# Six up-projection steps of each feed-forward layer, done as seven products of quarters

## The chip, the cores and the metric

The kernel runs on one core of one Trainium2 chip. The metric is the device time of one execution in microseconds (us), as a median over runs; a profiled execution gives the trace, in which every instruction of the five engines has its start and its duration. PE is TensorE (matrix products), DVE is VectorE, ACT is ScalarE, POOL is GpSimd, and SP is SyncE, which here issues most DMA transfers.

## The reference

One inference step of a two-layer decoder trunk for 512 prompt tokens, 16 learned tokens in front of them, and 8 x 4 tokens of a sample group. Each layer is a mixer (linear attention with RWKV-7 in layer 0, gated DeltaNet in layer 1) and a feed-forward block, each followed by a layer norm. The change touches the feed-forward block alone:

```
x <- LN(alpha*x + ConvFFN(x))
ConvFFN: W_down( silu(causal_dwconv3(x W_gate)) * (x W_up) )
D_MODEL = 1024    D_FF = 2816    FFN_CONV = 3
```

## The kernel before

The block of a layer is written by `ffn`. Features lie on the 128 partitions and tokens along the free axis: 560 columns in layer 0, 548 in layer 1. D_FF is worked through in 22 steps f of 128 features, and these in three parts (`PARTS`): f = 0 to 7, 8 to 15, 16 to 21. A step computes `pg` (the gate) and `pu` (the up projection) of x. Matrix products are made in three terms, since each operand is held as a high and a low half: `xh`, `xl` for x, `wh`, `wl` for a weight (`split`: the high half by a cast on ACT, the low half by a subtraction, as a rule on DVE). A projection is thus 8 tiles along the 1024 inputs x 3 terms x 2 halves of the columns = 48 matmuls. Its weights come by one DMA of 512 KB into a `wraw` tile; `fetch` has three of these slots, and SP's next fetch waits for the slot of the third one back to be read.

After the products of a step, ACT copies `pg` from PSUM to `gp`; three DVE instructions make the convolution (`ac`), ACT the tanh (`th`), DVE the rest of silu and the product with `pu` (`h`), and ACT and DVE split it into `hh` and `hl`. POOL copies the carried rows in and out (`cn`, `gp`). After each part the down projection adds up over the part's features: 8 output tiles `pd` of 48 matmuls each, which DVE adds into the residual `r`. After part 0, POOL sums the tiles of `r`, and in step f = 12 a mean is taken off them (8 POOL subtractions). Up to four PSUM tiles of two banks each are in use. The first two steps' products are made inside the layer norm before (`lead`; their weights are `vh`, `vl`), so that pg and pu of f = 2 are the first ones that `ffn` issues itself.

Order on each engine is set by a scheduler that goes by priority, in the order of the code; `later` and the new `sooner` shift that priority.

Of the kernel before, what the change touches and what calls it, by code (L numbers as in the profile page):

```python
# [12 lines left out]
F32 = mybir.dt.float32  # L13
# [8 lines left out]
KT = 8  # L22
# [26 lines left out]
class K:  # L49
    def __init__(self, ctx, tc, a, o):  # L50
        self.ctx, self.tc, self.nc, self.a, self.o = ctx, tc, tc.nc, a, o
        self.cp = ctx.enter_context(tc.tile_pool(name="const", bufs=1))
        self.table = False
        self.rp = ctx.enter_context(tc.tile_pool(name="rp", bufs=1))
        self.wp = ctx.enter_context(tc.tile_pool(name="wp", bufs=2))
        self.nw, self.every = 0, 1
        self.cut = KT
        self.side, self.rate, self.credit, self.pre, self.raw, self.lo = None, 0, 0, [], [], None

    def consts(self):  # L60
# [66 lines left out]
    def weights(self, src, k):  # L127
        return self.pre.pop(0) if self.pre else self.prepared(src, k)
# [218 lines left out]
def h2(ap, n=280):  # L347
    return ap.rearrange("p (h c) -> p h c", c=n)
# [14 lines left out]
LAST = Span(12)  # L363


def ffn(k, l, sn, xh, xl, r, pp, lead, nxt):
    nc, tc = k.nc, k.tc
    P, N, C, G = sn.pr, sn.nt, sn.c, sn.pr + 2
    E = G + 46
    with ExitStack() as es:  # L370
        sp = es.enter_context(tc.tile_pool(name=f"ffn{l}", bufs=2))
        hp = es.enter_context(tc.tile_pool(name=f"ffnh{l}", bufs=1))
        cs = hp.tile([128, NFF, 8, 2], F32, name="cs")
        nc.scalar.dma_start(cs, k.a["s_ffn"][l])
        cn = hp.tile([128, NFF, 9, 2], F32, name="cn")
        hh = hp.tile([128, KT, N], F32R, name="hh")
        hl = hp.tile([128, KT, N], F32R, name="hl")
        ln = LN(k, es, f"f{l}", sp, pp, r, sn)
        for f0, nf in PARTS:
            for j in range(nf):  # L380
                f = f0 + j
                if f == PARTS[1][0] + 4:
                    pc = pp.tile([128, 2, 512], F32, tag="pj", name="pc")
                    for i, (c, m) in enumerate(sn.halves):
                        nc.tensor.matmul(pc[:, i, 0:m], k.o1024, total[:, c : c + m], start=True, stop=True)
                    nc.scalar.copy(h2(total, sn.w), pc[:, :, 0 : sn.w])
                    for m in range(KT):
                        nc.gpsimd.tensor_sub(r[:, m, 0:N], r[:, m, 0:N], total)
                if lead:
# [15 lines left out]
                nc.vector.tensor_scalar(ac[:, 0:E], gp[:, 0:E], w(0), k.v(f"fb{l}", f), op0=ALU.mult, op1=ALU.add)  # L405
# [8 lines left out]
                nc.vector.scalar_tensor_tensor(  # L414
                    h2(h[:, 0:P], C), h2(th[:, 0:P], C), 0.5, pu[:, :, 0:C], op0=ALU.mult, op1=ALU.mult
                )
                nc.vector.scalar_tensor_tensor(
                    h[:, P:N].rearrange("p (b c) -> p b c", c=4),
                    th[:, G : G + 48].rearrange("p (b c) -> p b c", c=6)[:, :, 0:4], 0.5,
                    pu[:, 1, C : C + NS].rearrange("p (b c) -> p b c", c=4), op0=ALU.mult, op1=ALU.mult,  # L420
                )
                k.split(h, hh[:, j], hl[:, j])
            src = lambda m: k.a["w_down"][l, m][:, f0 : f0 + nf]
            if f0 + nf < NFF:
                for m in range(KT):
# [36 lines left out]
class LN:  # L462
# [58 lines left out]
    def add(self, h, s, p, ps):  # L521
        k, nc, r, w = self.k, self.k.nc, self.r, self.sn.w
        x = r[:, 2 * p : 2 * p + 2, s]
        nc.vector.scalar_tensor_tensor(x, x, self.alpha, ps[:, :, 0:w], op0=ALU.mult, op1=ALU.add)
        if p == 1:
            nc.gpsimd.tensor_add(self.sum, r[:, 0:2, s], x)
            (q0, _), (q1, _) = self.square(s, 0), self.square(s, 1)
            nc.vector.tensor_add(self.sq[h], q0, q1)
        elif p == 2:
            nc.gpsimd.tensor_add(self.sum, self.sum, x)  # L530
            nc.vector.tensor_add(self.sq[h], self.sq[h], self.square(s, p)[0])
            nc.gpsimd.tensor_add(self.sum[:, 0], self.sum[:, 0], self.sum[:, 1])
            nc.vector.tensor_add(self.sq[h][:, 0], self.sq[h][:, 0], self.sq[h][:, 1])
# [1427 lines left out]
```

## Time and profile before

| | |
|---|---|
| median of 3 runs | 1909.08 us (1909.01 to 1911.29) |
| profiled execution, its own time | 1901.78 us |
| its span in the trace | 1900.0 us |
| PE busy | 1794.4 us, 94% |
| DVE, ACT, POOL busy | 62%, 40%, 25% |

The span runs from the first to the last instruction of the trace; the 1.8 us beside it lie around the program. The profiled execution is 7.3 us shorter than the median of the other runs, so sums are made as differences and then put on the median. The steps that `ffn` issues itself and the down projections of parts 0 and 1 lie at 567 to 916 us of the span in layer 0 and at 1502 to 1847 us in layer 1.

### The profile page before, as it was taken

Reading aid. Unit: us, or ns where it says so; the run is one execution under the profiler, and the core shown is the slowest. Engines: PE = TensorE matmul, PEld = TensorE weight load, DVE = VectorE, ACT = ScalarE, POOL = GpSimd, SP = SyncE. Lnnn points to the kernel's source line nnn. Section 1 sums busy time; section 2 is a strip of 40 time slices with the busy share of each in tenths; the row PEclk is TensorE's granted clock in tenths of the full one; section 3 lists DMA queues with packets and bytes.
Section 4 is the critical chain, followed back from the end, with each engine's and each line's share of the span. In section 5 each row is a group of like instructions: output and inputs, shape, how many; then the busy total and the mean of one; then the engine's idle time right before and its main releaser. Section 6 shows DMA issues by size and latency. Waiting matters only on the chain.

```text
span 1900.0 us, 34370 instructions
## 1 busy us (share of the span) xinstructions
PE 1794.4 (94%) x13901; PEld 1679.7 (88%) x13901; DVE 1184.1 (62%) x2047; ACT 754.7 (40%) x1393; POOL 482.4 (25%) x750
## 2 busy tenths in 40 slices
PE   8999999798899999999988999899978999999997
PEld 7887888676899999999987997898768999999996
DVE  5757444546785556535766887688578654564466
ACT  6453423435353223223446454444344432232233
POOL 1333343313430113000131433333143201130002
PEclk9999999889899999999998999899898999999998
DMA  6110222301412222323321112421333122222231
GB/s 208 45 45 25 59 84 65 118 23 40 163 52 78 79 89 78 90 89 92 116 72 54 65 40 73 138 64 47 103 122 100 49 80 88 89 82 86 90 105 48
DMA packets 67358, 153.64 MB, mean 81 GB/s; under 512 B 15656, under 2 KB 26728, under 8 KB 67200
## 3 DMA queue, kind: packets, MB, share of 16 engines
q1 hardware_dynamic: 62784, 142.68, 24.3%
q10 hardware_dynamic: 3104, 4.15, 0.7%
q0 software_dynamic: 1312, 4.63, 0.6%
q8 instruction: 109, 1.79, 0.4%
q14 instruction: 49, 0.40, 0.1%
HBM read 136.72 MB, written 14.70 MB: 80 GB/s over the span
## 4 chain that ended last, share of the span: by engine, by line
PE 79%; DVE 9%; issue 4%; ACT 4%; DMA 2%; POOL 2%; SPq 0%; POOLq 0%; DVEq 0%; ACTq 0%
PE pd L162 17%; PE pu L162 13%; PE pg L162 13%; PE ph L162 12%; PE lead L162 3%; PE p L786 2%; PE pm L952 2%; PE px L740 1%; PE pw L756 1%; PE psr L286 1%; PE pt L750 1%; DVE ac L1534 1%; DVE r L566 1%; DVE r L1909 1%; PE psm L259 1%
## 5 line engine op out<-in xcount | busy, mean ns | idle before, releaser
L109 ACT CAST wh<-wraw 128x1024 fp32r<-128x1024 f32 x177 | 185.0, 1045 | 442.4 <-issue 156.2
L110 DVE TENSOR_TENSOR wl<-wraw,wh 128x1024 fp32r<-128x1024 f32 x156 | 210.0, 1346 | 177.6 <-ACT wh L109 177.1
L162 PE MATMUL ph<-xh,wh 128*128 128x280 f32 (+3 forms) x864 | 266.8, 309 | 9.4 <-ACT wh L109 6.1
L162 PE MATMUL ph<-xh,wl 128*128 128x280 f32 (+3 forms) x864 | 264.1, 306 | 0.4 <-DVE wl L110 0.4
L162 PE MATMUL ph<-xl,wh 128*128 128x280 f32 (+3 forms) x864 | 263.8, 306 | 0.0
L162 PE MATMUL pg<-xh,wh 128*128 128x264 f32 (+3 forms) x640 | 186.6, 292 | 0.0
L162 PE MATMUL pu<-xh,wl 128*128 128x264 f32 (+3 forms) x640 | 186.4, 291 | 0.0
L162 PE MATMUL pg<-xh,wl 128*128 128x264 f32 (+3 forms) x640 | 186.4, 291 | 0.0
L162 PE MATMUL pu<-xh,wh 128*128 128x264 f32 (+3 forms) x640 | 186.2, 291 | 0.0
L162 PE MATMUL pu<-xl,wh 128*128 128x264 f32 (+3 forms) x640 | 186.0, 291 | 0.0
L162 PE MATMUL pg<-xl,wh 128*128 128x264 f32 (+3 forms) x640 | 186.0, 291 | 0.0
L162 PEld LDWEIGHTS ph<-xh,wh 128*128 128x128 f32 x864 | 166.8, 193 | 16.9 <-ACT wh L109 7.2
L162 PEld LDWEIGHTS ph<-xl,wh 128*128 128x128 f32 x864 | 166.7, 193 | 5.6 <-issue 3.6
L162 PEld LDWEIGHTS ph<-xh,wl 128*128 128x128 f32 x864 | 166.4, 193 | 5.0 <-issue 3.6
L162 PE MATMUL pd<-hl,wh 128*128 128x280 f32 (+1 forms) x512 | 148.8, 291 | 0.1
L162 PE MATMUL pd<-hh,wl 128*128 128x280 f32 (+1 forms) x512 | 148.7, 291 | 0.0
L162 PE MATMUL pd<-hh,wh 128*128 128x280 f32 (+1 forms) x512 | 147.9, 290 | 0.0
L401 POOL COPY cn<-gp 128x2 f32<-128x2 f32 x44 | 31.1, 707 | 437.4 <-ACT gp L399 437.4
L162 PEld LDWEIGHTS pg<-xl,wh 128*128 128x128 f32 x640 | 121.0, 189 | 0.1
L162 PEld LDWEIGHTS pu<-xl,wh 128*128 128x128 f32 x640 | 121.0, 189 | 0.0
L162 PEld LDWEIGHTS pg<-xh,wh 128*128 128x128 f32 x640 | 120.9, 189 | 0.1
L162 PEld LDWEIGHTS pu<-xh,wh 128*128 128x128 f32 x640 | 120.9, 189 | 0.0
(566 smaller groups left out, 4751.0 us busy)
## 6 DMA issues: line engine op xcount, KB each, us to landing
wraw<-in_w_up SPq DMA_DIRECT2D x88, 512.0 KB, 3.5
wraw<-in_w_down SPq DMA_DIRECT2D x32, 512.0 KB, 3.5
wraw<-in_w_c SPq DMA_DIRECT2D x32, 512.0 KB, 3.6
wraw<-in_w_ab SPq DMA_DIRECT2D x26, 512.0 KB, 3.7
wraw<-in_w_down SPq DMA_DIRECT2D x16, 384.0 KB, 3.3
wraw<-in_w_oab SPq DMA_DIRECT2D x8, 512.0 KB, 4.0
sb<-in_s_gdn SPq DMA_DIRECT2D x16, 256.0 KB, 2.7
so<-in_s_gdn SPq DMA_DIRECT2D x16, 256.0 KB, 3.0
```

What stands on the lines that cost most here:

```text
L109: self.nc.scalar.copy(hi, src)
L110: (eng or self.nc.vector).tensor_sub(lo, src, hi.bitcast(F32))
L162: self.nc.tensor.matmul(ps[:, :m], a[:, i, :], x[:, i, c : c + m], start=(i == 0 and n == 0), stop=(i == k - 1 and n == 2))
L259: last = self.nc.tensor.matmul(ps[:, :m], lhsT, rhs[:, c : c + m], start=True, stop=True)
L286: k.nc.tensor.matmul(ps, z[:, 64 * b : 64 * b + 64], s[:, b % 4], start=(b == 0), stop=(b == 7))
L401: nc.gpsimd.tensor_copy(cn[:, f, 0, :], gp[:, P:G])
L566: st(t, t, k.v(g, m), rs, op0=ALU.mult, op1=ALU.mult)
L740: nc.tensor.matmul(px[:L, i, :L], a16[:L, i, :L], T[:L, i, :L], start=True, stop=True)
L750: nc.tensor.matmul(pt[:L, i, :L], W[:L, i, :L], X[:L, i, :L], start=not ta, stop=True)
L756: nc.tensor.matmul(pw[:L, i, :L], X[:L, i, :L], W[:L, i, :L], start=not wa, stop=True)
L786: nc.tensor.matmul(t[:L, i:e], a(h0 + i), y, start=(j == 0), stop=(j == len(terms) - 1))
L952: mm(pms[h][:L, n, :, :L], x[hs, tl], d["ra"][hs, :, tl], start=True, stop=True)
```

## The change

From f = 5 on, every other step of parts 0 and 1 (f = 5, 7, 9, 11, 13, 15, in each layer) no longer calls `proj` for `pg` and `pu`. The weights of gate and up projection form a 2 x 2 matrix of blocks (two outputs by two halves of the 1024 inputs), and x one of 2 x 2 blocks (two halves of the inputs by two halves of the columns). Strassen's scheme in Winograd's form makes the product of the two with seven block products in place of eight. A block product is 4 tiles x 3 terms = 12 matmuls of 280 columns (274 in layer 1), in a PSUM tile `pv` of its own. What the scheme needs beside them:

- once a layer (`sums`, emitted behind step f = 2): four differences of quarters of x, in two pieces each: 8 POOL instructions of 128x560, 8 ACT casts, and 8 low halves, 4 each on DVE and POOL;
- for each such step (`weights`): four sums or differences of half weights on POOL (128x512), 7 high halves on ACT, 6 low halves on DVE and one on POOL;
- for each such step (`products`): the seven tiles are emptied by 2 ACT copies and 6 DVE additions (the one behind the sixth product in two pieces), with 2 more additions on POOL, all at a priority 400 earlier (`sooner`).

The first tap of the convolution goes from DVE to ACT in these steps. The sums over `r` are now made after part 1 in place of part 0, in a tile `k.mid`, and the mean is taken off in step f = 18 in place of f = 12; the layer norm's pools are opened after part 1.

```diff
+    @contextmanager
+    def sooner(self):
+
+        tc = self.tc
+        p = tc.cur_priority
+        tc.cur_priority = p - 400
+        yield
+        tc.cur_priority = p
...
+    def sums(self):
...
+        ts = [tuple(self.xp.tile([128, 4, w], F32R, name=f"x{n}{i}") for n in "hl") for i in range(4)]
+        for j in (0, 2):
+            y = lambda a, b: x(a, b)[:, j : j + 2]
+
+            def diff(i, eng, p, q):
+                t = self.sp.tile([128, 2, 280], F32, tag="sum", name="xt")[:, :, 0:w]
+                eng.tensor_sub(t, p, q)
+                k.split(t, *(p[:, j : j + 2] for p in ts[i]), nc.gpsimd if i % 2 else None)
+                return t
+
+            t1 = diff(0, nc.gpsimd, y(0, 1), y(0, 0))
+            t2 = diff(1, nc.gpsimd, y(1, 1), t1)
+            diff(2, nc.gpsimd, y(1, 1), y(0, 1))
+            diff(3, nc.gpsimd, y(1, 0), t2)
...
+        s1 = both(True, h(u, 0), h(u, 1))
+        a11, c2 = room()
+        k.split(h(g, 0), *a11)
+        s2 = both(False, s1, h(g, 0))
+        k.split(s2, *c2)
+        a12, c1 = room()
+        k.split(h(g, 1), *a12, gp)
+        k.split(s1, *c1)
+        s4 = both(False, h(g, 1), s2)
+        s3 = both(False, h(g, 0), h(u, 0))
+        c3, c4 = room()
+        k.split(s3, *c3)
+        k.split(s4, *c4)
+        a22, = room(1)
+        k.split(h(u, 1), *a22)
...
+        def product(wt, xt):
+            ps = pp.tile([128, 2, 512], F32, tag="pj", name="pv")[:, 0, 0:w]
+            terms = [(wt[a][:, i], xt[b][:, i]) for i in range(4) for a, b in ((0, 0), (0, 1), (1, 0))]
+            for n, (p, q) in enumerate(terms):
+                nc.tensor.matmul(ps, p, q, start=n == 0, stop=n == 11)
+            return ps
...
+        ps = product(a11, self.b11)
+        with k.sooner():
+            nc.scalar.copy(c11, ps)
+        ps = product(s2, t2)
+        with k.sooner():
+            add(u2, ps, c11)
...
+        ps = product(a22, t4)
+        with k.sooner():
+            add(u3, ps, u3)
...
-                if f == PARTS[1][0] + 4:
+                if f == PARTS[2][0] + 2:
...
+                seven = SV <= f < PARTS[2][0] and f % 2
...
+                if f == 2:
+                    sv.sums()
```

ACT's order where `ffn` of layer 0 begins, before the change. `gp<-lead`, `th` and `hh` belong to f = 0 and 1; the `wh` in the last row but two is the high half for pg of f = 3.

```order
L246 ACTIVATE th<-ac 128x576
L399 COPY gp<-lead 128x528
L400 COPY gp<-lead 128x8x4
L109 CAST hh<-h 128x560
L246 ACTIVATE th<-ac 128x576
L109 CAST hh<-h 128x560
L109 CAST wh<-wraw 128x1024
L399 COPY gp<-pg 128x528
L400 COPY gp<-pg 128x8x4
```

The same place with the change; `xt` are the differences of x that POOL makes, `xh_65..` their high halves.

```order
L119 CAST hh<-h 128x560
L119 CAST xh_6513<-xt 128x560
L256 ACTIVATE th<-ac 128x576
L119 CAST xh_6515<-xt 128x560
L119 CAST xh_6517<-xt 128x560
L119 CAST xh_6519<-xt 128x560
L119 CAST hh<-h 128x560
L119 CAST xh_6513<-xt 128x560
L119 CAST xh_6515<-xt 128x560
L119 CAST xh_6517<-xt 128x560
L119 CAST wh<-wraw 128x1024
L531 COPY gp<-pg 128x528
```

Seven casts of differences now stand ahead of the weights' cast for pg of f = 3, one of them ahead of the tanh of f = 1 and six behind it. On POOL, the differences and low halves stand at that place in this order (nothing like them stood there before, only the four small rows of copies per step):

```order
L401 TENSOR_TENSOR xt<-r,xt 128x560
L401 TENSOR_TENSOR xt<-r 128x560
L528 MEMSET gp 128x2
L529 COPY gp<-cs 128x8x2
L401 TENSOR_TENSOR xt<-r,xt 128x560
L120 TENSOR_TENSOR xl_6516<-xt,xh_6515 128x560
L401 TENSOR_TENSOR xt<-r 128x560
L120 TENSOR_TENSOR xl_6520<-xt,xh_6519 128x560
L401 TENSOR_TENSOR xt<-r,xt 128x560
L401 TENSOR_TENSOR xt<-r 128x560
L120 TENSOR_TENSOR xl_6516<-xt,xh_6515 128x560
L401 TENSOR_TENSOR xt<-r,xt 128x560
```

One more difference, the first, stands ahead of these rows; the last row but two is the ninth of the large ones, counted with it, and its cast is the last that ACT makes ahead of the weights of f = 3.

DVE's order in part 1 of layer 0, before the change: one normal step, from the low half of the weights to that of h.

```order
L110 TENSOR_TENSOR wl<-wraw,wh 128x1024
L405 TENSOR_SCALAR ac<-gp,vec 128x576
L407 SCALAR_TENSOR_TENSOR ac<-gp,vec,ac 128x576 x2
L412 SCALAR_TENSOR_TENSOR th<-th,ac 128x576
L414 SCALAR_TENSOR_TENSOR h<-th,pu 128x528
L417 SCALAR_TENSOR_TENSOR h<-th,pu 128x32
L110 TENSOR_TENSOR wl<-wraw,wh 128x1024
L110 TENSOR_TENSOR hl<-h,hh 128x560
```

The same stretch with the change, from the end of a normal step (f = 12) into the following step of seven (f = 13). The rows with 128x512 are low halves for the seven products, those with `pv` empty their tiles.

```order
L120 TENSOR_TENSOR wl<-ws,wh 128x512 x2
L120 TENSOR_TENSOR hl<-h,hh 128x560
L464 TENSOR_TENSOR u_8434<-pv,gp 128x280
L120 TENSOR_TENSOR wl<-wraw,wh 128x1024
L467 TENSOR_TENSOR gp<-pv,gp 128x280
L473 TENSOR_TENSOR u_8436<-pv,u_8434 128x280
L478 TENSOR_TENSOR gp<-pv,u_8434 128x248
L478 TENSOR_TENSOR gp<-pv,u_8434 128x8x4
L120 TENSOR_TENSOR wl<-ws,wh 128x512
L120 TENSOR_TENSOR wl<-wraw,wh 128x1024
L482 TENSOR_TENSOR u_8436<-pv,u_8436 128x280
L542 SCALAR_TENSOR_TENSOR ac<-gp,vec,ac 128x576
```

A pair of steps thus keeps its two long `wl` rows and gets six short ones and six additions from PSUM for the two long rows and the tensor-scalar row that the step of seven drops; the `wl` of the next pg (fourth row) now stands behind the first addition, and so behind the second product.

## Rows read from the trace of the kernel before

**Rows 1.** The page: span, busy time by engine.

```profile
span 1900.0 us, 34370 instructions
PE 1794.4 (94%) x13901; PEld 1679.7 (88%) x13901; DVE 1184.1 (62%) x2047; ACT 754.7 (40%) x1393; POOL 482.4 (25%) x750
```

**Rows 2.** Stretches of both blocks: PE, PEld, DVE, ACT, POOL busy, PEclk, DMA.

```profile
567.00:916.00 349.00, 348.97 (x2699) 348.34 (x2698) 185.59 (x221) 101.10 (x144) 44.60 (x93) 1.00 0.29 89
1502.00:1847.00 345.00, 344.96 (x2701) 344.35 (x2700) 183.96 (x219) 99.64 (x144) 44.30 (x93) 1.00 0.29 88
```

**Rows 3.** The chain that ended last: start, duration, piece.

```profile
567.16 6.21 PE pg L162 x48
...
579.58 6.21 PE pg L162 x48
...
641.64 2.94 PE pd L162 x23
...
644.60 46.63 PE pd L162 x361
...
1578.94 46.28 PE pd L162 x361
...
1643.56 6.12 PE pu L162 x48
```

**Rows 4.** Timeline of ACT and DVE where the block of layer 0 begins.

```profile
573.31 1.05 ACT L109 CAST wh<-wraw 128x1024 fp32r<-128x1024 f32 x1 [2.28 <-PE pg L162]
574.39 1.23 DVE L110 TENSOR_TENSOR wl<-wraw,wh 128x1024 fp32r<-128x1024 f32 x1 [2.58 <-ACT wh L109]
576.15 1.67 DVE L407 SCALAR_TENSOR_TENSOR ac<-gp,vec,ac 128x576 f32<-128x576 f32 x2
578.57 0.76 DVE L412 SCALAR_TENSOR_TENSOR th<-th,ac 128x576 f32<-128x576 f32 x1 [0.75 <-ACT th L246]
```

**Rows 5.** Timeline of POOL and DVE around step f = 12 and in part 0's end.

```profile
692.14 1.39 POOL L434 TENSOR_TENSOR lnsum<-lnsum,r 128x560 f32<-128x560 f32 x1 [4.78 <-DVE r L429]
692.22 2.40 DVE L110 TENSOR_TENSOR wl<-wraw,wh 128x1024 fp32r<-128x1024 f32 x1 [0.22 <-ACT wh L109]
...
743.03 13.16 POOL L388 TENSOR_TENSOR r<-r,lnsum 128x560 f32<-128x560 f32 x8 [3.55 <-ACT lnsum L386]
...
749.05 2.46 DVE L110 TENSOR_TENSOR wl<-wraw,wh 128x1024 fp32r<-128x1024 f32 x1 [5.28 <-ACT wh L109]
751.43 1.64 DVE L405 TENSOR_SCALAR ac<-gp,vec 128x576 f32<-128x576 f32 x1
753.11 3.70 DVE L407 SCALAR_TENSOR_TENSOR ac<-gp,vec,ac 128x576 f32<-128x576 f32 x2
```

**Rows 6.** Groups by shape: busy us, mean ns of one; and DMA issues of the page.

```profile
L109 ACT CAST hh<-h 128x560 fp32r<-128x560 f32 x20 | 13.1, 655 | 3.3 <-DVE h L417 3.3
L1742 POOL TENSOR_TENSOR so<-so,egs 128x512 f32<-128x512 f32 x16 | 17.8, 1127 | 26.8 <-DMA so<-in_s_gdn 12.2 <-DVE r L1781 6.5 <-DVE wl L110 5.5
wraw<-in_w_up SPq DMA_DIRECT2D x88, 512.0 KB, 3.5
```

**Rows 7.** Windows with gaps of PE; columns as in rows 2.

```profile
516.00:518.00 2.00, 0.00 (x0) 0.00 (x0) 1.33 (x4) 0.00 (x0) 1.00 (x1) 1.00 0.55 223
...
956.00:958.00 2.00, 0.00 (x0) 0.00 (x0) 1.97 (x3) 0.21 (x1) 2.00 (x3) 1.00 0.00 0
958.00:960.00 2.00, 0.24 (x1) 0.27 (x2) 1.84 (x4) 0.67 (x1) 0.56 (x1) 1.00 0.00 0
960.00:962.00 2.00, 2.00 (x9) 1.65 (x9) 0.45 (x1) 0.09 (x1) 0.00 (x0) 0.64 0.00 0
962.00:964.00 2.00, 2.00 (x11) 2.00 (x11) 0.59 (x2) 1.28 (x3) 0.00 (x0) 0.51 0.00 0
```

**Rows 8.** Timeline of ACT and DVE at the end of part 0.

```profile
642.54 0.66 ACT L109 CAST hh<-h 128x560 fp32r<-128x560 f32 x1
643.81 0.73 DVE L110 TENSOR_TENSOR hl<-h,hh 128x560 fp32r<-128x560 f32 x1
```

More of the change, by code (lines that the diff above doesn't have):

```diff
@@ L28 @@
 PARTS = ((0, 8), (8, 8), (16, 6))
+SV = 5
 TILES = [(0, 112), (112, 112), (224, 112), (336, 96), (432, 128)]
@@ L363, with __init__, weights, both @@
 LAST = Span(12)
+class Seven:
+    def __init__(self, k, es, name, xh, xl, r, w):
+        self.k, self.w, self.x = k, w, (xh, xl, r)
+        pool = lambda n, bufs=1: es.enter_context(k.tc.tile_pool(name=f"sv{name}{n}", bufs=bufs))
+        self.xp, self.sp, self.tp = pool("x"), pool("s", 3), pool("t")
+        self.wps, self.n = (pool("w", 2), k.wp), 0
+    def sums(self):
+        k, nc, w = self.k, self.k.nc, self.w
+        xh, xl, r = self.x
+        x = lambda a, b: r[:, 4 * a : 4 * a + 4, b * w : b * w + w]
+        part = lambda a, b: (xh[:, 4 * a : 4 * a + 4, b * w : b * w + w], xl[:, 4 * a : 4 * a + 4, b * w : b * w + w])
+        self.b11, self.b21, self.b22 = part(0, 0), part(1, 0), part(1, 1)
+        ts = []
+        ts = [tuple(self.xp.tile([128, 4, w], F32R, name=f"x{n}{i}") for n in "hl") for i in range(4)]
[10 more added lines that the diff above has]
+            diff(3, nc.gpsimd, y(1, 0), t2)
+        self.t = ts
+    def weights(self, g, u):
+        k, gp = self.k, self.k.nc.gpsimd
+        h = lambda raw, i: raw[:, 4 * i : 4 * i + 4]
+        def both(add, p, q):
+            t = self.sp.tile([128, 2, 280], F32, tag="sum", name="ws").rearrange("p a b -> p (a b)")[:, 0:512]
+            t = t.rearrange("p (a b) -> p a b", b=128)
+            (gp.tensor_add if add else gp.tensor_sub)(t, p, q)
+            return t
+        def room(n=2):
+            self.n += 1
+            w = [self.wps[self.n % 2].tile([128, KT, 128], F32R, tag=t, name=t) for t in ("wh", "wl")]
+            return [[t[:, 4 * i : 4 * i + 4] for t in w] for i in range(n)]
+        s1 = both(True, h(u, 0), h(u, 1))
[13 more added lines that the diff above has]
+        k.split(h(u, 1), *a22)
+        return a11, a12, c2, c1, c3, c4, a22
+    def products(self, pp, src_g, src_u, c11, c12):
+        k, nc, w = self.k, self.k.nc, self.w
+        g, u = k.fetch(src_g, KT), k.fetch(src_u, KT)
+        a11, a12, s2, s1, s3, s4, a22 = self.weights(g, u)
+        t1, t2, t3, t4 = self.t
+        def product(wt, xt):
[4 more added lines that the diff above has]
+            return ps
+        u2, p5, u3 = (self.tp.tile([128, 280], F32, tag=t, name=t)[:, 0:w] for t in ("u2", "p5", "u3"))
+        add, also = nc.vector.tensor_add, nc.gpsimd.tensor_add
+        ps = product(a11, self.b11)
[4 more added lines that the diff above has]
+            add(u2, ps, c11)
+        ps = product(a12, self.b21)
+        with k.sooner():
+            add(c11, ps, c11)
+        ps = product(s1, t1)
+        with k.sooner():
+            nc.scalar.copy(p5, ps)
+        ps = product(s3, t3)
+        with k.sooner():
+            add(u3, ps, u2)
+            also(u2, u2, p5)
+        ps = product(s4, self.b22)
+        with k.sooner():
+            for t, c, m in c12:
+                add(t, m(ps[:, c]), m(u2[:, c]))
+            also(p5, p5, u3)
+        ps = product(a22, t4)
+        with k.sooner():
+            add(u3, ps, u3)
+        return u3, p5
@@ L377, in ffn @@
         hl = hp.tile([128, KT, N], F32R, name="hl")
-        ln = LN(k, es, f"f{l}", sp, pp, r, sn)
+        total = k.mid[:, 0:N]
+        e2 = ExitStack()
+        sv = Seven(k, e2, f"{l}", xh, xl, r, sn.w)
         for f0, nf in PARTS:
@@ L388, in ffn @@
                         nc.gpsimd.tensor_sub(r[:, m, 0:N], r[:, m, 0:N], total)
-                if lead:
+                seven = SV <= f < PARTS[2][0] and f % 2
+                gp = sp.tile([128, 578], F32, tag="gp", name="gp")
+                gs = gp[:, G : G + 48].rearrange("p (b c) -> p b c", c=6)
+                W, by4 = sn.w, lambda x: x.rearrange("p (b c) -> p b c", c=4)
+                if seven:
+                    same, p = lambda x: x, P - W
+                    g1, g2, g3 = gp[:, 2 : 2 + W], gp[:, 2 + W : G], gs[:, :, 2:6]
+                    cu, cv = sv.products(
+                        pp, k.a["w_up"][l, 2 * f], k.a["w_up"][l, 2 * f + 1],
+                        g1, [(g2, slice(0, p), same), (g3, slice(p, W), by4)],
+                    )
+                elif lead:
                     pg, pu = lead.pop(0), lead.pop(0)
@@ L404, in ffn @@
                 ac = sp.tile([128, 578], F32, tag="ac", name="ac")
-                nc.vector.tensor_scalar(ac[:, 0:E], gp[:, 0:E], w(0), k.v(f"fb{l}", f), op0=ALU.mult, op1=ALU.add)
+                if seven:
+                    nc.scalar.activation(ac[:, 0:E], gp[:, 0:E], AF.Identity, scale=w(0), bias=k.v(f"fb{l}", f))
+                else:
+                    nc.vector.tensor_scalar(ac[:, 0:E], gp[:, 0:E], w(0), k.v(f"fb{l}", f), op0=ALU.mult, op1=ALU.add)
                 for t in (1, 2):
@@ L429, in ffn @@
                     st(h2(r[:, m, 0:N], sn.w), h2(r[:, m, 0:N], sn.w), 1.0 if f0 else ALPHA, pd[:, :, 0 : sn.w], op0=ALU.mult, op1=ALU.add)
-                if f0 == 0:
-                    total = ln.sum.rearrange("p h c -> p (h c)")
+                if f0:
+                    e2.close()
+                    ln = LN(k, es, f"f{l}", sp, pp, r, sn)
                     nc.gpsimd.tensor_add(total, r[:, 0, 0:N], r[:, 1, 0:N])
```

23 lines of the change are left out of this document (11 added, 12 removed).

## The prediction

> **What bounds the kernel now.** The page first: PE is busy 94% of the span, DVE 62%, ACT 40%, POOL 25% [rows 1]. A share is a mean over unlike stages, so the stretches that the change touches are read next. In both feed-forward blocks PE is busy for all but 0.03 or 0.04 us, at the granted clock of 1.00, while DVE works 186 of 349 us and POOL 45 [rows 2]. The chain of waits there is PE alone: 48 matmuls of a projection in 6.21 us in layer 0 and 6.12 in layer 1, and the matmuls of the down projection with no break [rows 3]. So a matmul less is time gained, as long as everything that feeds PE keeps up; and each wait that the change gives PE is lost in full, for PE has no idle time there in which to make up for it.
>
> **What it removes.** A step had 96 matmuls, 12.41 us (2 x 6.21) or 12.24 (2 x 6.12). It now has 84, all of 280 columns (274 in layer 1). The down projection's matmuls are of just that width: 46.63/361 = 0.1292 us and 46.28/361 = 0.1282 us each [rows 3]. So 10.85 and 10.77 us: a gain of 1.56 and 1.47 us per step, and with six steps per layer 9.4 + 8.8 = 18.2 us. This is the largest gain possible.
>
> **What it adds, first: the sums of x.** Where the block begins, the last lead matmul ends at 567.16, and pg of f = 3 begins 12.42 us later, at 579.58 [rows 3]. Its weights were ready long before: cast at 573.31, low half at 574.39 + 1.23 = 575.62 [rows 4]. Now seven casts of differences stand ahead of that cast on ACT, and the last of them needs POOL's ninth large instruction. POOL can't begin before 567.16, since the first difference goes into space that the lead's weights free. A POOL instruction on two operands of 128x560 takes 1.39 us (the single one at 692.14) or, in a row of eight beside DVE, 13.16/8 = 1.65 [rows 5]. So the ninth ends at 579.7 to 582.0. Behind it come one cast (0.66) [rows 6], the weights' cast (1.05), and the low half on DVE, 1.23 [rows 4] or 2.46 where POOL runs beside it [rows 5]: 582.6 to 586.2. PE wants it at its third matmul, 579.58 + 0.26 = 579.84. The wait is 2.8 to 6.3 us in layer 0, and as much in layer 1, where the order is the same. Between these ends I take 5.5, near the upper one, because three more large POOL instructions stand behind the ninth and meet DVE just there. If the POOL work were spread over a longer time, none of this would be there; what used to hide the cast is ACT's idle 2.28 us ahead of it [rows 4], which is gone.
>
> The clock adds to it. A gap of 2 us left the granted clock at 1.00, a gap of some 3.8 us was followed by 4 us at 0.64 and 0.51 of full speed, the lower of the two levels (1.2 GHz) for most of them: (0.36 + 0.49) x 2 = 1.7 us lost [rows 7]. A wait of 5.5 is past that, so 1.7 more; bounds 0 and 1.7. Together 7.2 per layer, 14.4 us in all; bounds 5.6 and 16.0.
>
> The price of contention is what decides here. With POOL's eight subtractions beside it, a low half took 2.46 us for 1.23, and two convolution taps 3.70 for 1.67 [rows 4, 5]: a DVE instruction gets 1.0 to 1.2 us longer when it meets a POOL instruction. The Trainium skill, page "SBUF — State Buffer", section "Who interferes with whom", says that a DVE instruction with two SBUF inputs contends with a GpSimd instruction that reads SBUF, and that the later one is blocked until the other is through. The rows agree. By a rule that GpSimd work is free beside DVE the sum below would be the 1901 of the first rival; by this one it is the forecast.
>
> **Second: the loop through the weights' slots.** In part 1 a normal step and a step of seven alternate, 12.41 + 10.85 = 23.26 us of PE. DVE's new order closes a circle that long: the fetch of the next step of seven's second weight waits until DVE has read the pg weights of the normal step ahead of it out of their slot; behind the fetch come POOL's sums, these are split on ACT and DVE between all the other work, and the pg weights of the next normal step stand behind the second product's addition, which needs those low halves. One turn, with rows 4 to 6 and 8: the transfer 3.5; POOL's sum 1.1, its cast 0.5 and low half 0.7; then on DVE the pu weights 1.2, an addition 0.4, two taps 1.7, a low half 0.7; tanh 0.75, th 0.8, h 1.0, hh 0.7 and hl 0.7; the normal step's three taps 2.2 and two low halves 1.4; tanh 0.75, th 0.8, h 0.9; two low halves 1.4, hl 0.7; the addition 0.4 and the pg weights 1.2. Half-width instructions, which the trace before lacks, are put at half of the full ones and a little more; the additions from PSUM at 0.4. The sum is 23.5 us: no slack against 23.26. Seven POOL instructions on two operands per turn, 1.13 each at 128x512 [rows 6], meet this DVE row. Each that does costs DVE about 1.1; if two or three fall on the circle, a turn takes 26. The first of the three turns from f = 9 to 15 has a slack of its own, since the pair is entered with weights fetched ahead. That leaves two turns, each 0 to 2.7 us late: 0 to 5.4 a layer. I take 2.5, 5.0 us for both.
>
> **Third: the ends of parts.** f = 7 and f = 15 are the last of their parts, and both are steps of seven. Before, h's high half came at 642.54 + 0.66 and its low one at 643.81 + 0.73 = 644.54 [rows 8], and 23 matmuls of the down projection, 2.94 us, covered the time from the last product to it [rows 3]. Now the gate is whole only after the sixth product, and then: addition 0.8, first tap 0.7, two taps 1.7, tanh 0.75, th 0.8, h 1.0, hh 0.7, hl 0.7, and 1.0 between engines, about 8.1 us, of which the seventh product covers 1.55. The order shows 42 matmuls of the down projection ahead of the first that needs this h, 5.4 us; the wait is about 8.1 - 1.55 - 5.4 = 1.1. I take 0.9, four times: 3.6 us; bounds 0, and 2.2 each if one instruction of the row meets POOL.
>
> **At nothing.** The mean moved from f = 12 to 18 is 8 POOL subtractions, 13.2 us [rows 5], that delay DVE there as they did before; four normal steps, 49 us, hide them. The sums over r run beside the down projection as before. ACT's 7 half casts and the tap, about 4.5 us more per step, are hidden in its idle time, 70% of the stretch [rows 2]. The seven PSUM tiles are emptied a product or two before PE comes back to them; where that cover is gone, each costs PE an addition, 0.4.
>
> **The sum.** -18.2 + 14.4 + 5.0 + 3.6 = +4.8 us. The profiled execution of 1901.78 would become 1906.6, and the median of 1909.1 becomes 1913.9. Between the bounds: -18.2 + 5.6 + 0 + 0 = -12.6, and -18.2 + 16.0 + 10.8 + 8.8 = +17.4.
>
> **The rivals.** (a) POOL and DVE hardly meet: the sums cost only their 2.8 us and a part of the clock, the loop is just closed, the ends cost 0.9. Then -18.2 + 6.6 + 0 + 3.6 = -8.0, 1901. For it speaks that DVE has idle time between its pieces, 163 of 349 us [rows 2]; against it, that in the one place where POOL works in a row every DVE instruction shown is late [rows 5]. (b) Nothing waits: 1909.1 - 18.2 = 1890.9. It needs the ninth POOL instruction by about 577, eight in 10 us; the fastest row gives 11.1. (c) DVE becomes the bound of part 1, and the change ends well on the slower side: DVE's own row per pair is about 18 us, and if five of the seven POOL instructions each add 1.1, the circle takes 28 to 29, so that every turn of the loop is late by some 5 us. Two turns in two layers: -18.2 + 16.0 + 20 + 3.6 = +21, 1930. It decides from the point where a turn is over 25 us; against it, that half of POOL's instructions fall in DVE's waits for tanh. (d) The change does not do what it says: the tiles are emptied no sooner, because additions stand in DVE's row behind low halves that wait for POOL. In the order shown the second product's addition stands behind two low halves and hl, so this is part of the loop; by itself, at 0.4 to 1.2 us for each of twelve steps, it would put 5 to 14 us on (a), 1906 to 1915.
>
> **How the numbers follow.** Forecast (1906 to 1921): 0.46. (a) 0.27, (b) 0.03, (c) 0.13, (d) alone 0.11. This measurement can tell a change of 0.2%, 3.8 us, from none: below 1905.3 is faster, above 1912.9 slower. Of the forecast's chance 0.03 lies below that bound (its lower tail), 0.12 within and 0.31 above; of (a) 0.25 below and 0.02 within; (b) is faster, (c) slower; of (d) 0.07 lies within and 0.04 above. This gives faster 0.31, same 0.21, slower 0.48. The range takes (a)'s middle and up to the forecast's end, with a part of (c): 1898 to 1925. Within the forecast by itself it would be 1907 to 1921.
>
> **What would show it.** A wait of PE for the low half of the weights at pg of f = 3, 4 to 6 us, and a granted clock below 1.00 behind it, in both layers; waits of PE for pg weights in f = 12, 14, or for the first low half of f = 13 and 15; waits of about 1 us for hh or hl where the down projections of parts 0 and 1 begin; products of 1.55 us each; DVE low halves of 128x512 above 1.5 us beside POOL's sums. Wrong would be the first term if the POOL rows at 567 end by 577; the second if DVE's row in part 1 shows idle time ahead of the pg weights; the whole if PE runs through both blocks as in rows 2.

## The result and the profile after

The median went from 1909.01 us (1906.74 to 1911.29, 5 runs) to 1918.09 us (1916.82 to 1922.43, 5 runs): the quotient of the two medians is 1.0048, and the ratio estimated from the runs is 1.0058, with a 95% interval of 1.0037 to 1.0078. The change makes the kernel 9 to 11 us slower, in the range forecast and on the side forecast.

The two profiled executions are further apart than that: 1919.9 us of span against 1900.0. The page of the changed kernel:

```profile
span 1919.9 us, 34470 instructions
PE 1800.1 (94%) x13757; PEld 1678.5 (87%) x13757; DVE 1272.8 (66%) x2175; ACT 796.2 (41%) x1481; POOL 632.9 (33%) x858
```

PE has 144 matmuls less than in [rows 1] and is busy longer; POOL works 150 us more, DVE 89. But 13.3 us of the difference in span lie ahead of the first feed-forward block, where the change moves nothing: the last lead matmul ends at 580.46 in place of 567.16 [rows 3]. The mean granted clock of that stretch was 0.92 in this execution and 0.96 in the one before the change, and PE was busy there for 540.5 us against 523.6 with the same 4024 matmuls; the stretch differs as much among the profiled executions of the experiments, which do the same work there (it ends at 568.3 in e1 and at 586.0 in e7). So the blocks are measured by themselves, from the end of the last lead matmul to the start of the last 127 matmuls of the down projection. First before the change, then after; the columns are those of rows 2.

```profile
567.16:937.05 369.89, 369.85 (x2859) 368.87 (x2857) 197.88 (x237) 107.96 (x153) 48.56 (x96) 1.00 0.29 89
1502.54:1868.14 365.60, 365.54 (x2858) 364.61 (x2857) 194.47 (x235) 104.90 (x150) 47.98 (x96) 1.00 0.28 83
```

```profile
580.46:960.70 380.24, 367.99 (x2786) 364.01 (x2785) 238.94 (x301) 128.41 (x197) 123.67 (x150) 0.98 0.28 86
1521.00:1887.49 366.49, 359.63 (x2785) 357.64 (x2785) 239.19 (x299) 125.56 (x194) 124.64 (x150) 0.99 0.28 83
```

Layer 0's block takes 10.4 us more, layer 1's 0.9 us: +11.2 together, in keeping with the +9.1 of the medians. PE, busy throughout before, now idles for 12.3 and 6.9 us, and the granted clock is no longer 1.00. The same two lengths are given for every experiment below.

What PE waited for in the blocks (waits of PE: us in total, times, longest), layer 0 and then layer 1. A wait costs some 0.3 us more than the idle time listed, since the matmuls beside it start later too: at the first wait for hh, listed with 0.39 us, two matmuls start 0.68 and 0.24 us behind the ones ahead of them, for 0.13 as a rule.

```profile
PE pg L172 <- ACT wh L119: 4.9, 1, 4.9
PE pv L454 <- ACT wh L119: 1.8, 2, 1.3
PE pg L172 <- DVE wl L120: 1.8, 1, 1.8
PE pu L172 <- DVE wl L120: 1.7, 1, 1.7
PE pv L454 <- DVE wl L120: 0.8, 4, 0.2
PE pd L172 <- ACT hh L119: 0.8, 2, 0.4
PE pd L172 <- DVE hl L120: 0.5, 2, 0.2
...
PE pg L172 <- ACT wh L119: 3.7, 1, 3.7
PE pg L172 <- DVE wl L120: 2.0, 1, 2.0
PE pd L172 <- ACT hh L119: 0.7, 2, 0.4
PE pd L172 <- DVE hl L120: 0.5, 2, 0.2
```

The largest is where the forecast put it, at pg of f = 3 in both layers. Its chain in layer 0, on the timelines of POOL, ACT and DVE:

```profile
580.55 1.92 POOL L401 TENSOR_TENSOR xt<-r 128x560 f32<-128x560 f32 x1 [2.34 <-PE lead L172]
...
585.75 0.10 POOL L528 MEMSET gp<- 128x2 f32 x1
585.79 0.70 POOL L529 COPY gp<-cs 128x16 f32<-128x16 f32 x1
...
594.68 1.36 POOL L401 TENSOR_TENSOR xt<-r 128x560 f32<-128x560 f32 x1
...
596.08 0.66 ACT L119 CAST xh<-xt 128x560 fp32r<-128x560 f32 x1 [0.67 <-POOL xt L401]
596.64 1.04 ACT L119 CAST wh<-wraw 128x1024 fp32r<-128x1024 f32 x1
...
597.89 2.39 DVE L120 TENSOR_TENSOR wl<-wraw,wh 128x1024 fp32r<-128x1024 f32 x1
```

POOL's ninth large instruction ends 15.6 us after the lead's last matmul (596.04 against 580.46), ACT casts its result, then the weights; DVE's low half takes 2.39 us beside POOL, for 1.23 alone [rows 4]. The two small rows at 585.75, which prepare `gp`, stand in POOL's order between the third large instruction and the fourth. And the clock around it:

```profile
594.00:596.00 2.00, 0.00 (x0) 0.00 (x0) 0.00 (x0) 0.66 (x1) 2.00 (x2) 0.88 0.00 0
596.00:598.00 2.00, 0.27 (x1) 0.27 (x2) 1.23 (x2) 1.92 (x3) 2.00 (x3) 0.50 0.00 0
...
604.00:606.00 2.00, 2.00 (x12) 2.00 (x11) 1.63 (x4) 1.20 (x3) 0.00 (x0) 0.56 0.04 8
606.00:608.00 2.00, 2.00 (x17) 2.00 (x16) 1.72 (x2) 0.63 (x1) 0.00 (x0) 1.00 0.00 0
```

The granted clock falls to the lower of its two levels (1.2 GHz) while PE waits and stays there for some five us after the weights have come, so that pg of f = 3 takes 11.2 us from first to last matmul, for 6.4 (1.8 of them are the wait for the low half). Apart from the waits for hh and hl at the ends of parts, the rest of the loss sits in layer 0 alone: at pu of f = 4, and in and around the steps of seven f = 7, 11, 13 and 15. Behind the wait at f = 13 the clock falls once more, to 0.60 and 0.54 in 776 to 780 us. These losses are read below, with the experiments.

### The profile page after: what moved, and what is told of

Read it like the earlier page. It is cut to its first block, busy times and chain, and to the rows that moved or that the text cites. A ratio compares the mean times of both kernels' runs of the same rounds, so it can differ in the third digit from the quotient of the medians.

```text
span 1919.9 us, 34470 instructions
## 1 busy us (share of the span) xinstructions
PE 1800.1 (94%) x13757; PEld 1678.5 (87%) x13757; DVE 1272.8 (66%) x2175; ACT 796.2 (41%) x1481; POOL 632.9 (33%) x858
## 5 line engine op out<-in xcount | busy, mean ns | idle before, releaser
L119 ACT CAST wh<-wraw 128x1024 fp32r<-128x1024 f32 (+1 forms) x189 | 181.5, 964 | 326.8 <-PE pd L172 129.6
L120 DVE TENSOR_TENSOR wl<-wraw,wh 128x1024 fp32r<-128x1024 f32 (+1 forms) x156 | 215.5, 1382 | 74.8 <-ACT wh L119 74.3
L172 PE MATMUL pu<-xh,wl 128*128 128x264 f32 (+3 forms) x448 | 130.7, 292 | 1.7 <-DVE wl L120 1.7
L172 PE MATMUL pu<-xh,wh 128*128 128x264 f32 (+3 forms) x448 | 130.3, 291 | 0.0
L172 PE MATMUL pu<-xl,wh 128*128 128x264 f32 (+3 forms) x448 | 130.2, 291 | 0.0
L120 POOL TENSOR_TENSOR wl<-wraw,wh 128x1024 fp32r<-128x1024 f32 (+1 forms) x32 | 66.6, 2083 | 184.6 <-ACT wh L119 181.7
L454 PE MATMUL pv<-xh,wh 128*128 128x280 f32 (+1 forms) x336 | 98.7, 294 | 1.8 <-ACT wh L119 1.8
L454 PE MATMUL pv<-xh,wl 128*128 128x280 f32 (+1 forms) x336 | 98.7, 294 | 0.8 <-DVE wl L120 0.8
L454 PE MATMUL pv<-xl,wh 128*128 128x280 f32 (+1 forms) x336 | 98.3, 293 | 0.0
L172 PEld LDWEIGHTS pd<-hh,wh 128*128 128x128 f32 x512 | 96.1, 188 | 2.4 <-ACT hh L119 2.4
```

What stands on the lines that cost most here:

```text
L119: self.nc.scalar.copy(hi, src)
L120: (eng or self.nc.vector).tensor_sub(lo, src, hi.bitcast(F32))
L172: self.nc.tensor.matmul(ps[:, :m], a[:, i, :], x[:, i, c : c + m], start=(i == 0 and n == 0), stop=(i == k - 1 and n == 2))
L454: nc.tensor.matmul(ps, p, q, start=n == 0, stop=n == 11)
```

## The experiments

They are numbered in the order in which they ran, and there is no e3. All run beside the kernel before; times are medians, ratios are to the kernel before with their 95% interval. "Blocks" are layer 0 + layer 1, measured as above.

| run | time | ratio | blocks | sum |
|---|---|---|---|---|
| before | 1908 to 1910 | 1 | 369.9 + 365.6 | 735.5 |
| changed | 1918.1 | 1.0058 [1.0037, 1.0078] | 380.2 + 366.5 | 746.7 |
| e1 x sums on POOL | 1923.3 | 1.0077 [1.0055, 1.0099] | 383.7 + 369.5 | 753.2 |
| e2 no x sums | 1897.9 | 0.9940 [0.9915, 0.9966] | 368.4 + 358.3 | 726.8 |
| e4 even steps | 1917.4 | 1.0045 [1.0023, 1.0067] | 380.0 + 366.8 | 746.8 |
| e5 no early priority | 1920.1 | 1.0050 [1.0030, 1.0069] | 381.2 + 366.7 | 747.9 |
| e6 no weight sums | 1910.9 | 1.0011 [0.9995, 1.0027] | 371.7 + 366.3 | 738.0 |
| e7 x sums alone | 1927.0 | 1.0096 [1.0070, 1.0121] | 379.5 + 373.9 | 753.4 |
| e8 e1, small rows on DVE | 1924.8 | 1.0078 [1.0062, 1.0094] | 384.5 + 368.8 | 753.3 |
| e9 e8, even steps | 1930.1 | 1.0102 [1.0070, 1.0135] | 386.8 + 370.9 | 757.8 |
| e10 e1, small rows on ACT | 1922.2 | 1.0073 [1.0051, 1.0096] | 381.9 + 365.4 | 747.3 |
| e11 up weight first | 1916.5 | 1.0036 [1.0017, 1.0055] | 375.9 + 367.0 | 742.9 |
| e12 e10 and e11 | 1919.4 | 1.0068 [1.0039, 1.0098] | 378.9 + 370.1 | 749.0 |
| e13 x sums on DVE, two pieces; e11 | 1895.6 | 0.9927 [0.9900, 0.9953] | 363.9 + 359.2 | 723.1 |

**Leaving the x sums out** (e2):

```diff
-        ts = [tuple(self.xp.tile([128, 4, w], F32R, name=f"x{n}{i}") for n in "hl") for i in range(4)]
-        for j in (0, 2):
+        ts = [self.b11, self.b21, self.b22, part(0, 1)]
+        for j in ():
```

> The x sums are left out (the products take quarters of x as they are, so the output is not the reference's). Theory: everything that PE waits for at f = 3 and f = 4 goes, 18 to 20 us for both layers, and the time is 1897 to 1901, below the kernel before. Rival (part 1's loop or DVE's load is the main cost): the time falls by under 10 us and stays at 1908 or more.

19.9 us less in the blocks, 20 in the median: as the theory had it. With this one term gone the change is faster than the kernel before by 8.7 us in the blocks, so the seven products do bring PE what they were to bring, less about 10 us.

**The x sums alone** (e7): they are made, and no step is a step of seven.

```diff
-                seven = SV <= f < PARTS[2][0] and f % 2
+                seven = False
```

> The x sums are made in both layers, but no step is a step of seven: one part of the change alone, beside the moved mean. Theory (the sums cost PE what the second run's difference gives, whatever the products are): 18 to 21 us more than the kernel before, 1926 to 1930, with the same waits at pg of f = 3 as with the whole change. Rival (the wait belongs to the two together): under 10 us more, below 1919.

The blocks take 9.6 and 8.3 us more than before, 17.9 together, and the median 17.8. PE's waits at that place are those of the changed kernel to a tenth:

```profile
PE pg L172 <- ACT wh L119: 4.9, 1, 4.9
PE pg L172 <- DVE wl L120: 1.8, 1, 1.8
...
PE pg L172 <- ACT wh L119: 3.7, 1, 3.7
PE pg L172 <- DVE wl L120: 2.0, 1, 2.0
```

So the price of the x sums doesn't depend on the products. The waits are 6.7 and 5.7 us; the other 2.9 and 2.6 us are what is left for the clock (and the few tenths that a wait costs beside its idle time). (The further 2 us of e2 are the low half of pu in f = 4, which PE waited 1.7 us for in the changed kernel, and which neither e2 nor e7 has.)

**The x sums wholly on POOL** (e1):

```diff
-                k.split(t, *(p[:, j : j + 2] for p in ts[i]), nc.gpsimd if i % 2 else None)
+                hi, lo = (p[:, j : j + 2] for p in ts[i])
+                nc.gpsimd.tensor_copy(hi, t)
+                nc.gpsimd.tensor_sub(lo, t, hi.bitcast(F32))
```

> All 24 instructions of the x sums on POOL; ACT and DVE have none of them in their order. Theory (the wait at pg of f = 3 comes from the casts of the differences, which stand ahead of the weights' cast on ACT): PE waits for no weights at f = 3, the granted clock stays at 1.00 there, and the time falls by 16 to 20 us to 1898 to 1902. Rival (POOL and DVE meeting is the cost, whatever the order): POOL works longer beside DVE, the wait stays above 5 us a layer, 1912 or more.

The wait at pg of f = 3 is gone, as the theory said, but the time rose to 1923.3: the wait moved on to pu of f = 4, 9.2 us for its high half. Its chain starts on DVE:

```profile
600.83 3.02 DVE L542 TENSOR_SCALAR ac<-gp,vec 128x576 f32<-128x576 f32 x1 [7.46 <-POOL gp L531]
603.88 1.67 DVE L544 SCALAR_TENSOR_TENSOR ac<-gp,vec,ac 128x576 f32<-128x576 f32 x2
...
605.59 0.68 ACT L256 ACTIVATE th<-ac 128x576 f32<-128x576 f32 x1 [12.90 <-DVE ac L544]
```

The convolution of f = 3 waits for POOL's two small rows that prepare `gp` (0.1 and 0.2 us), which now stand behind 23 of the 24 long ones; the tanh waits for the convolution, and the next weights' casts stand behind the tanh. The expectation had named order as the cause and left out what else stands in POOL's order.

**The small rows on DVE** (e8): e1, and

```diff
-                nc.gpsimd.memset(gp[:, 0:2], 0.0)
-                nc.gpsimd.tensor_copy(gs[:, :, 0:2], cs[:, f])
+                small = nc.vector if f in (2, 3, 4) else nc.gpsimd
+                small.memset(gp[:, 0:2], 0.0)
+                small.tensor_copy(gs[:, :, 0:2], cs[:, f])
```

> The x sums wholly on POOL as in the first run, and the two small rows that prepare gp in steps f = 2, 3 and 4 on DVE, ahead of POOL's long row no longer waited for. Theory (order alone made both waits): PE waits for nothing between the lead steps and f = 5, the feed-forward blocks take about 727 us together as without the sums, and the time is 1898 to 1901. Rival (24 POOL instructions beside DVE still delay its low halves): a wait of over 3 us a layer remains at f = 4 or 5, 1904 or more.

The rival's numbers came, at another place: 1924.8, with a wait for a low half of 13.4 us in layer 0 and 8.4 in layer 1, at pu of f = 3, a step earlier than it said. One of the two rows on DVE's timeline, and POOL's in the same stretch:

```profile
599.62 6.46 DVE L532 COPY gp<-cs 128x16 f32<-128x16 f32 x1 [8.72 <-issue]
...
599.54 1.35 POOL L401 TENSOR_TENSOR xt<-r 128x560 f32<-128x560 f32 x1
...
605.40 0.64 POOL L403 CAST xh<-xt 128x560 fp32r<-128x560 f32 x1
606.12 1.84 POOL L404 TENSOR_TENSOR xl<-xt,xh 128x560 fp32r<-128x560 f32 x1
```

DVE first stood 8.7 us. The view names no releaser for this; POOL's copies out of `gp` end at 599.58, just ahead, so it was probably the slot of `gp` that DVE stood for. Then it needed 6.46 us for a copy of 16 elements a partition, which took 0.17 us at another place of this run: it came to an end at 606.08, in a pause of POOL of 0.08 us, after six of POOL's instructions. In layer 1 the same copy, also beside POOL's row, took 1.28 us.

**The same with even steps** (e9): e8, and SV = 4 with `f % 2 == 0`.

> As the run before, and the steps of seven are f = 4 to 14, so that none is the last of its part. Theory (the ends of parts cost 3 to 4 us on top): 2 to 4 us less than that run, 1895 to 1898, if the sums are ready for f = 4. Rival (the sums and f = 4's weight sums, behind them on POOL, are late by 2 us or more): the same as that run or slower.

1930.1, the slowest, as the rival had it: f = 4's weight sums stand behind POOL's long row, and a cast of one of them held ACT for 19.5 us, PE for 17.2. It tells of the row on POOL, and nothing of the parts' ends.

**The small rows on ACT** (e10): e1, and the copies into and out of `gp` of f = 1 to 4 by `nc.scalar`.

> The x sums wholly on POOL, and the small copies into and out of gp of steps f = 1 to 4 on ACT, so that no engine needs anything from POOL's long row before f = 5. Theory (what PE waited for was order and the small rows, DVE's own lengthening fits into its idle time): no wait of PE between the lead steps and f = 5 above 1 us, the blocks take about 727 us, time 1898 to 1902. Rival (POOL beside DVE for 33 us makes DVE late all by itself): a wait for a low half of over 3 us a layer, 1906 or more.

The rival came closer, in layer 0 for another reason than it gave. Up to pg of f = 4 there is no wait above 0.4 us. Then, at pu of f = 4, PE waits 8.2 us in layer 0, for a weights' cast that stands on ACT behind the cast of f = 5's first weight sum, which POOL makes after its long row:

```profile
620.64 0.62 ACT L119 CAST wh<-ws 128x512 fp32r<-128x512 f32 x1 [7.02 <-POOL ws L420]
621.16 1.04 ACT L119 CAST wh<-wraw 128x1024 fp32r<-128x1024 f32 x1
...
1558.97 2.28 DVE L120 TENSOR_TENSOR wl<-wraw,wh 128x1024 fp32r<-128x1024 f32 x1
```

In layer 1 it is the wait that the rival named: 3.6 us for the low half in the last row, which takes 2.28 us beside POOL and stands behind a convolution whose three instructions take 1.50, 1.06 and 1.80 us there.

Three times, then, the wait came back where the next thing stands behind POOL's row or meets it: it is POOL's total of some 35 us (582.36 to 618.0 in this run) that has no room ahead of f = 5.

**Even steps** (e4): `SV = 4`, `f % 2 == 0`, nothing else.

> The steps of seven are f = 4, 6, 8, 10, 12, 14 in place of 5 to 15, so none is the last of its part. Theory (the chain to h behind the sixth product is longer than the matmuls that cover it): no wait for hh, hl or the seventh product's weights at the ends of parts, 3 to 5 us less, 1913 to 1916; the sums are needed one step earlier, which may take some of it back. Rival (the ends cost nothing that matters): within 1 us of 1918.

The median is 0.7 us lower, within noise, and the blocks are the same. But the waits for hh and hl at the ends of parts, 1.3 and 1.2 us in the changed kernel, are gone from the list, and the down projections of parts 0 and 1 take 49.6 us each in layer 0, from their first matmul to the next pg, as before the change, for 50.5 in the changed kernel (49.2 for 50.1 in layer 1); the wait for the high half at pg of f = 3 grew from 4.9 to 6.1 us in layer 0 and from 3.7 to 4.9 in layer 1, and a wait for the low half of its pu comes in (2.1 and 1.6 us; 1.7 us at pu of f = 4 go in layer 0). Both halves of the expectation came true, and cancel.

**The normal priority** (e5): `p` in place of `p - 400` in `sooner`.

> The tiles of the products are emptied at the normal priority. Theory (the early priority keeps the PSUM tiles free): PE waits for a tile or for weights in steps of seven, 3 to 10 us more, 1921 to 1928. Rival (the tiles have slack, the priority does nothing): within 1 us of 1918.

1.2 us more in the blocks, 2 us in a median that scatters by as much: the early priority is worth little here. No wait for the emptying of one of the seven tiles stands in PE's list in either.

**No weight sums** (e6): `both` returns its first operand in place of a sum.

```diff
-            (gp.tensor_add if add else gp.tensor_sub)(t, p, q)
-            return t
+            return p
```

> The four sums of half weights per step of seven are left out: the splits take a half of the raw weight as it is (so the output is not the reference's); POOL has 24 instructions of 128x512 less per layer. Theory (in layer 0 the circle through slots, transfer, POOL's sums and the splits is a little longer than PE's pair): the waits of PE in steps of seven of part 1 in layer 0, about 5 us, go, in layer 1 nothing changes, 1912 to 1914. Rival (the circle is held by DVE's load alone, the sums are not on it): within 1.5 us of 1918.

8.5 us less in layer 0, 0.2 in layer 1. All of PE's waits in layer 0 between pg of f = 3 and the ends of parts are gone. So POOL's sums of weights are on the circle in layer 0, and in layer 1 they are not. Of the 8.5 us, 5.7 lie at f = 11 to 15, and 2.6 at f = 4 and f = 7, in part 0. The run takes away the time that the sums need and their meetings with DVE at once; it does not tell the two apart. The timelines tell the difference: first layer 0, then layer 1, both where the products of f = 11 end (the changed kernel; POOL, ACT, DVE).

```profile
762.97 1.29 POOL L418 TENSOR_TENSOR ws<-wraw 128x512 f32<-128x512 f32 x1 [2.53 <-DMA wraw<-in_w_up]
764.29 0.62 ACT L119 CAST wh<-ws 128x512 fp32r<-128x512 f32 x1 [6.34 <-POOL ws L418]
764.82 1.05 ACT L119 CAST wh<-wraw 128x1024 fp32r<-128x1024 f32 x1
765.90 2.00 DVE L120 TENSOR_TENSOR wl<-wraw,wh 128x1024 fp32r<-128x1024 f32 x1 [0.26 <-ACT wh L119]
...
1694.17 1.05 ACT L119 CAST wh<-wraw 128x1024 fp32r<-128x1024 f32 x1 [2.14 <-PE pv L454]
1695.26 1.23 DVE L120 TENSOR_TENSOR wl<-wraw,wh 128x1024 fp32r<-128x1024 f32 x1 [0.38 <-ACT wh L119]
1695.94 1.72 POOL L418 TENSOR_TENSOR ws<-wraw 128x512 f32<-128x512 f32 x1 [0.94 <-DMA wraw<-in_w_up]
1697.69 0.62 ACT L119 CAST wh<-ws 128x512 fp32r<-128x512 f32 x1 [1.71 <-POOL ws L418]
```

In layer 0 the scheduler put the cast of POOL's sum ahead of the cast of the pu weights: ACT stands 6.3 us, and the pu weights, the last product's addition and the convolution queue up behind a DMA. In layer 1 the pu weights go first, and the same work runs without a wait.

**The up weight first** (e11):

```diff
-        g, u = k.fetch(src_g, KT), k.fetch(src_u, KT)
+        u, g = k.fetch(src_u, KT), k.fetch(src_g, KT)
```

> As the changed kernel, but a step of seven fetches its up weight ahead of its gate weight, so that POOL's first sum need not wait for the later transfer. Theory (in layer 0 the circle of slot, transfer, sum, splits is what is late): layer 0's waits in steps of seven shrink from 6 us to under 2, nothing else changes, 1911 to 1915. Rival (the gate weight, now the later, is on the circle as much as the up weight was): within 2 us of 1918.

Layer 0's block is 4.4 us shorter, layer 1's 0.5 longer; the waits for weights in steps of seven of part 1 go from 2.4 to 0.2 us (and 0.9 us come in for the tile of a pu that DVE reads late). At pu of f = 4 the wait of 1.7 us goes too. The median, 1916.5, is within its scatter of both theories; the blocks speak for the first. (The 6 us that the expectation gives as waits in steps of seven are more than the list has: 2.6 there and 1.7 at f = 4; the 6 us fit the whole loss at f = 11 to 15, clock included.)

**Both** (e12): e10 and e11.

> Both edits of the two runs before. Theory: their gains add, 1892 to 1897, 12 to 17 us below the kernel before. Rival (one of them fails, or one's order undoes the other): no better than the better of the two.

The rival: the sums on POOL stay in the way (10.8 us at a pg in layer 0), whatever is fetched first.

**The x sums on DVE, in two pieces** (e13), with the up weight first:

```diff
-                k.split(t, *(p[:, j : j + 2] for p in ts[i]), nc.gpsimd if i % 2 else None)
+                k.split(t, *(p[:, j : j + 2] for p in ts[i]))
...
-            t1 = diff(0, nc.gpsimd, y(0, 1), y(0, 0))
+            t1 = diff(0, nc.vector, y(0, 1), y(0, 0))
...
-                if f == 2:
-                    sv.sums()
+                if f in (2, 3):
+                    sv.sums(2 * f - 4)
```

> The x sums wholly on DVE (16 instructions of 128x560) and ACT's casts, in two pieces behind f = 2 and f = 3, so that DVE's row has the weights' low half of f = 3 between them, about 9 us after the last lead matmul and some 3 us before PE wants it; the up weight is fetched first. POOL has nothing in that stretch. Theory (the sums' work itself has room on DVE and ACT; POOL's pace and the rows that wait for it were the cost): no wait of PE for weights ahead of f = 5, layer 0's waits in part 1 small, the blocks take 722 to 727 us together in place of 747, 1894 to 1900, faster than both kernels. Rival (16 more DVE instructions make DVE late in f = 2 to 4 as POOL did): waits of over 3 us a layer at f = 3 or 4, 1907 or more.

As the theory said. The blocks and PE's waits in them (layer 0, layer 1):

```profile
582.26:946.17 363.91, 361.56 (x2785) 359.51 (x2785) 243.85 (x313) 128.52 (x197) 109.27 (x138) 1.00 0.30 90
1506.43:1865.61 359.18, 357.19 (x2785) 355.38 (x2785) 236.23 (x311) 125.43 (x194) 107.73 (x138) 1.00 0.28 85
```

```profile
PE pd L172 <- ACT hh L119: 0.8, 2, 0.4
PE pv L453 <- DVE h L548: 0.8, 2, 0.6
PE pd L172 <- DVE hl L120: 0.5, 2, 0.3
...
PE pd L172 <- ACT hh L119: 0.7, 2, 0.4
PE pv L453 <- DVE h L548: 0.5, 1, 0.5
PE pd L172 <- DVE hl L120: 0.5, 2, 0.2
```

No wait is left at f = 3 or 4, the clock is 1.00, and the blocks take 12.4 us less than before the change: 1895.6 us, a ratio of 0.9927, faster than both kernels. DVE does no more in the blocks than it did in the changed kernel (480 us against 478), though 12 instructions a layer came to it from POOL: without POOL beside them its others are shorter (the low half of f = 3 takes 1.23 us, for 2.39).

## Why the prediction was right

The forecast was +4.8 us with a range up to 1925; the medians give +9.1, the blocks +11.2. The side and most places of the losses were foreseen; the size is about half of what was measured, because two of its terms are too small. By its steps:

**The gain.** Forecast 1.56 and 1.47 us per step. In layer 1 the chain that ended last has the 84 matmuls of a step of seven in 10.67 us, so 12.24 - 10.67 = 1.57; six steps in two layers make about 19 us for 18.2. Right.

```profile
1566.30 10.67 PE pv L454 x84
```

**The x sums.** Forecast 7.2 us per layer, at most 8.0; e7 shows 9.6 and 8.3. The mechanism, the place and the order of links were right. Two sizes were off. The ninth POOL instruction came at 15.6 us in layer 0, past the upper bound of 14.8, and at 14.2 in layer 1. In layer 0 the nine take 14.8 us by themselves, the dearer of the two prices, since they met DVE's (the first took 1.92 us, for 1.39); the other 0.8 are the two small rows for `gp` among them, which stand in the order shown ahead of the prediction and which its sum left out. So the wait for weights, forecast at 5.5, was 6.7 and 5.7. And the clock cost 2.6 to 2.9 us in place of 1.7. The gaps behind that price, read off windows of 2 us as 2 and 3.8 us, were 2.7 and 4.1 us by PE's idle time, and the lower level lasted 3.4 us behind the longer one; here PE stood twice in a row (4.9 and 1.8 us in layer 0), and the lower level lasted from 595.5 to 605.7. That the rows agree with the Trainium skill ("SBUF — State Buffer", "Who interferes with whom"), by which a DVE instruction with two SBUF inputs contends with a GpSimd instruction that reads SBUF, stands for this case: a low half took 2.39 us beside POOL here, for 1.23.

**The loop through the slots.** Forecast 2.5 us per layer. By e6 the weight sums cost layer 0 8.5 us, past the upper bound of 5.4, and layer 1 nearly nothing (0.2). At f = 11 to 15, where the term was worked out, it is 5.7 us; the 2.6 at f = 4 and f = 7 had no term. The circle was seen rightly in layer 0, e11 and e6 shorten it there, but the prediction worked it out for one order and took it for both layers, and it put the lateness on DVE's row, where the timelines show ACT standing 6.3 us for POOL's sum; PE then waited for a high half at f = 13 and 15, not for pg at f = 12 and 14. The layers differ in their order at the two rows shown above, among others; that these two rows decide is read from the timelines, and no run changed them alone. Why the scheduler chose otherwise in layer 1 was not tried. That the total of the term, 5.0 against about 8.7, is off by less than its parts is luck.

**The ends of parts.** Forecast 0.9 four times. The waits for hh and hl were 1.3 us in layer 0 and 1.2 in layer 1 for two ends each, so about 0.6 an end; with what a wait costs beside its idle time, each of these four down projections takes 0.9 us longer than before the change (50.47 us for 49.58 in layer 0, 50.12 for 49.24 in layer 1), and e4 takes just this away. Right. Together the three terms measure 17.9 + 8.7 + 3.5 = 30.1 us, against the 18.8 + 11.2 = 30.0 that the gain and the blocks ask for: nothing large is left without a cause.

**At nothing.** The moved mean and the emptying of the tiles cost nothing that shows: no run's waits in the blocks have one for them (the waits of up to 0.6 us for `h` in e11 and e13 are for the tile of a normal step's pu). ACT's extra casts show only through their place in the order.

**The rivals.** (a), POOL and DVE hardly meet, is wrong by the 2.39 us and by the 9.6 and 8.3 us of e7. (b) failed at its condition, a ninth instruction 10 us after the lead's end; it came after 15.6 and 14.2. (The prediction's 11.1 us there are eight instructions; nine at 1.39 make 12.5.) (c), DVE as the bound, would have shown as waits in every turn of both layers; layer 1 has none. (d) is half right: additions did stand behind low halves that waited for POOL, in layer 0, but e5 shows that the priority had little to do with it, and PE waited for none of the seven tiles.

What stays open: how e13 would divide between its edits, since the x sums on DVE were run neither with the old order of fetches nor in one piece. By e11 the order of fetches is worth 4 us in layer 0; the other 20 or so would belong to DVE in place of POOL and the two pieces together.

## What to carry to other kernels

A saving on the engine that bounds is lost where its new by-work stands, in an engine's order, ahead of something that this engine needs soon. Look not at how long the by-work takes but at what stands behind each of its instructions on every in-order engine; when it is moved to another engine, read that engine's small rows too. Three moves here took one wait away and made another, because the slow engine's total had no room ahead of its user, whoever waited for it. The fourth gave the work to an engine whose load looked higher (DVE, 53% busy) but whose instructions are shorter (a difference takes 0.74 us there, for 1.36 to 1.92 on POOL) and were put in two pieces with the weights' low half of f = 3 between them. Which of these mattered most was not tried.

## What was not expected of the hardware

A DVE copy of 128x16 took 6.46 us in e8, and 6.45 us in e9 at the same place of layer 0 (for f = 4), beside a row of POOL instructions with no pause of 0.1 us; ahead of POOL's row it took 0.17 us. DVE instructions on two operands in SBUF lost 1.0 to 1.2 us each beside POOL [rows 5], and this copy lost about as much at its other places beside POOL's row: it took 0.92 to 1.15 us for f = 3, and 1.28 us at the same place of layer 1, in both runs. What kept it out for six POOL instructions in layer 0 is not shown.
